# Longer activation and weight buffers, and one half of a layer in products of 256 columns

## The chip, the core and the metric

The kernel runs on one core of a Trainium2 chip. It is one program: a transformer block with adaptive normalization, then two layers of a second model, on 512 tokens of 1,024 features. The metric is the time of one execution on the device in microseconds (us). Three runs of the kernel before took 1934.53, 1937.00 and 1937.11 us; the median is 1937.0 us.

## The reference

Everything is float32. `x` is [512, 1024] after dropping the batch of one, and all weights come from memory.

```python
# block one: adaptive norm, two attentions, gates, an MLP
h      = modulate(rmsnorm(x, norm1_g), shift1, scale1)
proj   = h @ w_in                                  # 1024 -> 4352
merged = sigmoid(ga) * (swa(qa, ka, va) @ w_a) + sigmoid(gb) * (moba(qb, kb, vb) @ w_b)
x      = x + gate1 * (merged @ w_out)
h2     = modulate(rmsnorm(x, norm2_g), shift2, scale2)
x      = x + gate2 * (square(relu(h2 @ w_mlp_in)) @ w_mlp_out)   # 1024 -> 4096 -> 1024
x      = rmsnorm(x, final_g)
# block two: two layers
for layer in range(2):
    h = rmsnorm(x, mix_norm_g[layer])
    x = x + (even_mixer(h) if layer == 0 else odd_mixer(h))      # ends in a 1024 x 1024 product
    h = rmsnorm(x, mlp_norm_g[layer])
    x = x + square(relu(h @ mlp_w1[layer])) @ mlp_w2[layer]      # 1024 -> 4096 -> 1024
```

The three MLPs are most of the arithmetic: each has 64 tiles of 128 output features over 1,024 inputs.

## The kernel before

**Split products.** A float32 operand is written as a high part in the matmul's rounded format (`F32R`) and the rest as a low part: weights as `wH` and `wL`, activations as `aH` and `aL` (features on the partitions, 512 tokens along the row). `mm3` (line 198) issues three matmuls for each piece of 128 inputs: high weights by high activations, high weights by low activations, low weights by high activations. The weights are the stationary operand (128 columns, loaded before every matmul), the activations move through (512 columns).

**The loop of a product.** `gemm_t_steps` (line 212) goes over output tiles of 128 features. For each it loads a block of weights (`load_w`, line 178: a DMA into `wraw`, a copy on ScalarE into `wH`, a subtraction on VectorE into `wL`, three buffers of each), takes an accumulator `acc` in PSUM (three of them) and runs over eight pieces of inputs: 24 matmuls. Then the accumulator is evacuated. In two places the 512 tokens go by halves, in matmuls of 256 columns: in the first three tiles of the first MLP, and in the last tile of two products (`apart`). In the projections to keys and values (`gemm_n_steps`, line 246) the operands change places: the weights move and the activations stand still.

**The MLP** (`mlp`, line 828) has four chunks, `c` from 0 to 3. In each the first product makes eight hidden tiles from `H` (the tiles `aH0` to `aH7` and `aL0` to `aL7`); `ev` (line 834) applies relu and square and splits the result into two tiles of the pool `hd` (22 buffers). The second product takes these sixteen `hd` tiles and adds into the residual. So a chunk is 192 matmuls that read `aH` and `aL`, and then 192 that read `hd`. The MLP of block one is called at line 660, those of block two from `sq_mlp` (line 874, `layer` 0 and 1).

**What sets the order.** Within each engine the order is fixed when the program is built. TensorE takes its instructions in that order, and a load of weights goes ahead beside the matmul before it. In most of block one and in the mixers small attention matmuls are woven in among the long products by a planner with estimated times; in the MLPs there is nothing of that kind after the first 24 steps.

**Where the tiles lie.** Tiles lie at the same address in each of the 128 partitions. Counted modulo 256 bytes, the built program has them so (a tile of 512 float32 is 2,048 bytes long, a weight buffer 4,096, so all the buffers of a pool have one place):

| tiles | place before, modulo 256 |
|---|---|
| `aH0`-`aH7`, `aL0`-`aL7`, all `wH`, all `wL` | 128 |
| `hd` in the three MLPs | 64 |
| `s2` and `oh` in block one (inputs of the products `w_out`, `w_a`, `w_b`), and `S` and `PT`, which hold three blocks of weights in the first projections | 64 |
| `s2` in the last mixer: high part of the input of `od_out` | 224 |
| `v` in the last mixer: low part of that input; these buffers are 2,080 bytes apart | 224, 192, 160, 128, 96, 64, 32, 0 |

A slice of 128 weight columns or of 256 tokens begins at a multiple of 512 bytes, so it has the place of its tile.

Of the kernel before, what the change touches and what calls it, by code (L numbers as in the profile page):

```python
# [11 lines left out]
F32 = mybir.dt.float32  # L12
# [13 lines left out]
NEG = -1e30  # L26
LAT = 6.5
# [24 lines left out]
class Weave:  # L52
    """Places small dependent work on TensorE among the steps of long matrix products.

    A task is a generator: it emits one stage, then yields the TensorE time (us, estimated)
    before which its next stage should not stand in TensorE's queue, or a function that
    gives that time, or None while it isn't known."""
# [57 lines left out]
class Build:  # L115
# [62 lines left out]
    def load_w(self, src, n=1024, pools=None, pool_h=False, pool_l=False):  # L178
        nc = self.nc
        (hp, hn, hb), (lp, ln, lb) = pools or ((self.wp, "wH", 3), (self.wp, "wL", 3))  # L180
        r = self.wp.tile([P, 1024], F32, name="wraw", bufs=4)
        nc.sync.dma_start(r[:, :n], src)
        h = hp.tile([P, 1024], F32R, name=hn, bufs=hb)
        if pool_h:
            nc.gpsimd.tensor_scalar(h[:, :n], r[:, :n], 1.0, 0.0, op0=OP.mult, op1=OP.add)
        else:
            nc.scalar.activation(h[:, :n], r[:, :n], AF.Copy)  # L187
        l = lp.tile([P, 1024], F32R, name=ln, bufs=lb)
        (nc.gpsimd if pool_l else nc.vector).tensor_tensor(l[:, :n], r[:, :n], h[:, :n], op=OP.subtract)  # L189
        return h, l  # L190
# [21 lines left out]
    def gemm_t_steps(self, srcs, xs, evac, group=1, kt=KT, pool_l=(), ks=None, halves=False, last=None):  # L212
        """out^T tile m = W[:, 128 m:]^T x^T; srcs: one block [128, kt*128] per tile.

        halves: the first group goes over one half of the tokens first; last: evacuates the
        last tile instead of evac, half by half."""
        m = 0
        while m < len(srcs):
            g = group if m == 0 else 1
            ms = list(range(m, min(m + g, len(srcs))))  # L220
            ws = [self.load_w(srcs[i], kt * P, pool_l=i in pool_l or self.lean) for i in ms]
            accs = [self.acc() for _ in ms]
            lag = (0, 0, 3)
            ks = ks or range(kt)
            apart = last is not None and ms == [len(srcs) - 1]
            for c in HALVES if apart or (halves and m == 0) else (slice(0, NT),):
                if apart and c.start:
                    accs = [self.acc()]
                if c.start and not apart:
                    lag = (0, 3, 6)  # L230
                for _, b, i in sorted((i + lag[b], b, i) for i in range(kt) for b in range(len(ms))):
                    k = ks[i]
                    while xs[k] is None:
                        yield "wait"
                    s = slice(k * P, k * P + P)
                    h, l = ws[b]
                    self.mm3(accs[b][:, c], h[:, s], l[:, s], xs[k][0][:, c], xs[k][1][:, c], i == 0, i == kt - 1)
                    yield
                if apart:
                    last(c, accs[0])  # L240
            for i, acc in zip(ms, accs):
                if not apart:
                    evac(i, acc)
            m += len(ms)

    def gemm_n_steps(self, srcs, xs, evac):
        """out tile [128 tokens, 512] = x W; srcs: four blocks [128, 2 k tiles, 512]."""
        accs = [self.acc() for _ in range(3)] + [self.pg()]
        mm = self.mm
        for b in range(4):  # L250
            h, l = self.load_w(srcs[b], pool_l=self.lean)
            for i in range(4):
                t = slice(i * P, i * P + P)
                for kk in range(2):
                    k = 2 * b + kk
                    s = slice(kk * NT, kk * NT + NT)
                    xh, xl = xs[k]
                    mm(accs[i], xh[:, t], h[:, s], start=(k == 0), stop=False)
                    mm(accs[i], xl[:, t], h[:, s], start=False, stop=False)
                    mm(accs[i], xh[:, t], l[:, s], start=False, stop=(k == KT - 1))  # L260
                    yield
        for i in range(4):
            evac(i, accs[i])

    def act_hl(self, k):
        return (self.ap.tile([P, NT], F32R, name=f"aH{k}"), self.ap.tile([P, NT], F32R, name=f"aL{k}"))
# [6 lines left out]
    def rsqrt(self, out, a, eps):  # L273
        """out = (a + eps) ** -0.5 by Newton steps; small tiles, a may lie in PSUM."""
# [13 lines left out]
    def sumsq(self, src, k, tag="ssq", scale=1.0, apart=False):  # L288
        """adds the squares of tile k (features on partitions) to a running tile, or returns them."""
        nc = self.nc  # L290
        if k == 0:
            s = self.sm.tile([P, NT], F32, name=tag, bufs=1)
            nc.scalar.activation(s, src, AF.Square, scale=scale)
            self.cur[tag] = s
        else:
            q = self.sm.tile([P, NT], F32, name="sq", bufs=2)
            nc.scalar.activation(q, src, AF.Square, scale=scale)
            if apart:
                return q
            nc.vector.tensor_tensor(self.cur[tag], self.cur[tag], q, op=OP.add)  # L300

    def mean_rows(self, *parts, pool=None):
        """mean over features as PSUM [128, 512], the same in every partition."""
# [5 lines left out]
    def rstd_rows(self, ms, name="R"):  # L309
        """(ms + eps) ** -0.5 as SBUF [128, 512]."""  # L310
# [6 lines left out]
    def cols_of(self, R, pool=None):  # L317
        """[128 tokens, 4] columns of rows that are the same in every partition."""
# [8 lines left out]
    def modulate(self, x, k, R, A, shift, hl=None, c=slice(0, NT)):  # L327
        """x R A + shift of tile k, split."""
# [26 lines left out]
def block_one(B):  # L355
    nc, tc, a = B.nc, B.tc, B.a
    with ExitStack() as st:
# [25 lines left out]
        def ada_first(c):  # L383
            """128 columns of shift1 and of scale1, four row tiles at a time side by side on TensorE."""
# [16 lines left out]
        def ada_vec(c):  # L401
            """the same columns on VectorE."""
# [8 lines left out]
        def ada(part, cb):  # L411
            """512 columns of the modulation, on VectorE."""
# [41 lines left out]
        def ev_q(tiles, acc):  # L454
            """1/8 of two heads of 64 rows, each block of 128 queries back to front: for each head
            a tile with the high part in the head's own rows and the low part in the other ones."""
# [8 lines left out]
        def ev_k(tiles, acc):  # L465
            """for each of two heads a tile with the high part twice; the low parts of both in a third one."""
# [68 lines left out]
        def ev_g(m, acc):  # L535
            """sigmoid as exp(-ln(1 + exp(-x)))."""
# [43 lines left out]
        def ev_last(c, acc):  # L580
            """the last tile of the residual, by halves."""
# [60 lines left out]
    with ExitStack() as st:  # L642
        hp = st.enter_context(tc.tile_pool(name="hp", bufs=1))
        at = hp
        B.tmp = lambda: hp.tile([P, NT], F32, name="hd", bufs=22)
# [17 lines left out]
def flip_blocks(t):  # L663
    """columns of [128, 512] with each block of 128 back to front."""
# [3 lines left out]
def load_strips(B, at):  # L668
    """bucket of each distance as one-hot columns with the mask's rows, and the heads' biases."""
# [8 lines left out]
def bias_strips(B, at, oh):  # L678
    """masked bias by reversed distance, one row per head, in DRAM."""
# [10 lines left out]
def bias_tile(B, at, h, off, n):  # L690
    """[128 queries, n] additive bias of head h, already masked; the last query first."""
# [7 lines left out]
class Attention:  # L699
    """the two softmax attentions of block one, as tasks; heads share buffers, counted in free."""  # L700
# [18 lines left out]
    def head(self, key, h, b, q, k, strip, spans, qk_banks, pt_banks, times, sink=None):  # L719
        """P^T of one head; spans: first and last key of each query tile; banks: tiles that share a PSUM bank."""  # L720
# [107 lines left out]
def mlp(B, hp, w1, w2, H, upd, group=1, pool_l=(), during=None, mid=None, last=None):  # L828
    """during: called with each step's number in the first product, which goes over half of the tokens first; mid: called after it."""
    nc = B.nc  # L830
    for c in range(4):
        hs = []

        def ev(m, acc):
# [3 lines left out]
            hl = (hp.tile([P, NT], F32R, name="hd", bufs=22), hp.tile([P, NT], F32R, name="hd", bufs=22))  # L838
            B.split(hl, r)
            hs.append(hl)  # L840
        first = dict(group=group, pool_l=pool_l, halves=during is not None) if c == 0 else {}
        for i, _ in enumerate(B.gemm_t_steps([w1[c * 8 + m] for m in range(8)], H, ev, **first)):
# [3 lines left out]
        if mid is not None and c == 0:  # L846
            mid()
        B.gemm_t([w2[c * 8 + m] for m in range(8)], hs, lambda m, acc: upd(m, acc, c == 3),
                 last=last if c == 3 else None)
# [24 lines left out]
def sq_mlp(B, layer):  # L874
    nc, tc, a, X = B.nc, B.tc, B.a, B.X
    with ExitStack() as st:
# [24 lines left out]
        mlp(B, hp, a[f"mlp1_{layer}"], a[f"mlp2_{layer}"], H, upd, group=3, mid=norm, last=end if layer else None)  # L901


def even_mixer(B, ev, H):
# [11 lines left out]
    def stats():  # L916
        """rstd of both norms, and the end of the first one."""
# [56 lines left out]
    def gelu(t):  # L974
        """t <- gelu(t), tanh form: t * exp(-ln(1 + exp(-2 u)))."""
# [85 lines left out]
    def stick_head(j, b, As):  # L1061
        """A^T of one head, key tiles side by side, masked."""
# [27 lines left out]
    def split_y():  # L1090
        """parts of the result take the place of H once that is used up."""
# [37 lines left out]
def stick_scores(B, ev, q, k, z, h, l, tiles):  # L1129
    """masked scores of some key tiles, and log(1 + exp) of them in two parts."""  # L1130
# [22 lines left out]
def stick_weights(B, z, h, l, tiles):  # L1153
    """z <- exp(z - the sum over this key and the later ones), for some key tiles."""
# [285 lines left out]
```

## Time and profile before

| what | value |
|---|---|
| median of three runs | 1937.0 us |
| the same runs, lowest and highest | 1934.53 and 1937.11 us |
| span of the profiled execution, first to last instruction | 1936.0 us |
| instructions in it | 22136 |
| TensorE matmuls | busy 1898.4 us, 8570 matmuls |
| TensorE weight loads | busy 1501.6 us |
| VectorE, ScalarE, GpSimd | busy 1066.2, 767.3, 212.5 us |
| DMA | 197.43 MB, mean 102 GB/s |

No time of its own is listed for the profiled execution beside its span. The span of 1936.0 us lies 1.0 us under the median of the runs.

Two things have to be known to read the rows. Matmuls are pipelined, and the end of one is modelled: the duration of a matmul of 512 columns is shown as about 0.39 us, but the next one starts after some 0.23 us. What a matmul costs in a long product is therefore read from start to start, not from its duration. And a matmul in float32 that isn't of the rounded format is two matmuls in the trace.

### The profile page before, as it was taken

To read this page: it belongs to the slowest core of one execution; us is meant where nothing else is said; L and a number is where in the kernel's file an instruction comes from. 1 tells how busy PE (TensorE), PEld (TensorE's weight loads), DVE (VectorE), ACT (ScalarE), POOL (GpSimd) and SP (SyncE) were. 2 spreads that over 40 slices of the span, in tenths; PEclk is the share of its full clock that TensorE was granted. 3 is DMA by queue.
4 is the path that set the end of the run, shared out by engine and by line. 5 is a ranking of instruction groups with operands and counts; after the bars stand their busy time and mean duration, and the time that the engine had idled before them with its cause. 6 is when DMAs were issued, how large, how long until landed. Compare 5 with 4: busy or idle time off the path is not lost.

```text
span 1936.0 us, 22136 instructions
## 1 busy us (share of the span) xinstructions
PE 1898.4 (98%) x8570; PEld 1501.6 (78%) x8570; DVE 1066.2 (55%) x1571; ACT 767.3 (40%) x1246; POOL 212.5 (11%) x149
## 2 busy tenths in 40 slices
PE   6999999999999999999899999999999999999999
PEld 3777778888888887776688888888777888888887
DVE  4765668664434346667755445546745554454544
ACT  2455454342323244666634232233436343223231
POOL 1000010010000001325320201100201001210100
PEclk8999999999999999999999999999999999999999
DMA  6523258522223223211122322222231233223221
GB/s 233 165 55 104 89 170 261 188 88 89 97 98 98 89 96 115 66 55 55 44 88 98 98 92 96 96 98 90 89 108 44 77 101 106 97 89 98 98 98 66
DMA packets 61640, 197.43 MB, mean 102 GB/s; under 512 B 6904, under 2 KB 8490, under 8 KB 61536
## 3 DMA queue, kind: packets, MB, share of 16 engines
q1 hardware_dynamic: 57864, 190.34, 29.8%
q10 hardware_dynamic: 3672, 5.69, 1.1%
q8 instruction: 67, 1.10, 0.2%
q14 instruction: 37, 0.30, 0.1%
HBM read 193.86 MB, written 2.15 MB: 101 GB/s over the span
## 4 chain that ended last, share of the span: by engine, by line
PE 88%; DVE 7%; ACT 3%; issue 1%; DMA 1%; SPq 0%; DVEq 0%; ACTq 0%
PE acc L193 79%; PE pm L193 5%; PE pg L193 2%; PE po L193 1%; DVE s L1230 1%; DVE sl L1150 1%; PE pm L196 1%; DMA oh<-ada 1%; ACT wH L187 0%; DVE wL L189 0%; ACT sz L1168 0%; ACT se L1146 0%; ACT se L1147 0%; DVE ge L979 0%; DVE aL L335 0%
## 5 line engine op out<-in xcount | busy, mean ns | idle before, releaser
L187 ACT ACTIVATE wH<-wraw 128x1024 fp32r<-128x1024 f32 (+1 forms) x304 | 314.7, 1037 | 752.3 <-PE acc L193 683.0
L189 DVE TENSOR_TENSOR wL<-wraw,wH 128x1024 fp32r<-128x1024 f32 (+1 forms) x269 | 365.1, 1358 | 298.9 <-ACT wH L187 291.9
L193 PE MATMUL acc<-aH,wH 128*128 128x512 f32 (+1 forms) x1296 | 507.3, 392 | 5.5 <-ACT aH L334 5.0
L193 PE MATMUL acc<-aL,wH 128*128 128x512 f32 (+1 forms) x1296 | 502.2, 387 | 3.4 <-DVE aL L335 3.4
L193 PE MATMUL acc<-aH,wL 128*128 128x512 f32 (+1 forms) x1296 | 501.5, 387 | 0.0
L193 PE MATMUL acc<-hd,wH 128*128 128x512 f32 (+1 forms) x1552 | 483.2, 392 | 0.0
L193 PEld LDWEIGHTS acc<-hd,wH 128*128 128x128 f32 x1552 | 289.4, 187 | 70.8 <-issue 1.0
L193 PE MATMUL acc<-hd,wL 128*128 128x512 f32 (+1 forms) x776 | 304.0, 392 | 0.0
L193 PEld LDWEIGHTS acc<-aH,wH 128*128 128x128 f32 x1296 | 244.2, 189 | 62.7 <-issue 9.2
L193 PEld LDWEIGHTS acc<-aL,wH 128*128 128x128 f32 x1296 | 244.4, 189 | 53.8 <-DVE aL L335 4.3
L193 PEld LDWEIGHTS acc<-aH,wL 128*128 128x128 f32 x1296 | 244.4, 189 | 50.7 <-issue 1.2
L193 PEld LDWEIGHTS acc<-hd,wL 128*128 128x128 f32 x776 | 145.2, 187 | 35.2
L189 POOL TENSOR_TENSOR wL<-wraw,wH 128x1024 fp32r<-128x1024 f32 x38 | 96.2, 2536 | 675.7 <-ACT wH L187 654.7
L889 POOL TENSOR_TENSOR X<-X,up 128x512 f32<-128x512 f32 x48 | 69.9, 1456 | 573.2 <-DVE up L887 322.0
L887 DVE TENSOR_TENSOR up<-acc,R 128x512 f32<-128x512 f32 x63 | 43.6, 692 | 153.7 <-PE acc L193 153.7
L270 ACT ACTIVATE hd<-rl 128x512 fp32r<-128x512 f32 x96 | 60.6, 632 | 120.5 <-DVE rl L837 120.4
L271 DVE TENSOR_TENSOR hd<-rl,hd 128x512 fp32r<-128x512 f32 x96 | 66.3, 692 | 60.8 <-ACT hd L270 60.8
L655 DVE SCALAR_TENSOR_TENSOR X<-acc,mod,X 128x512 f32<-128x512 f32 x32 | 24.0, 751 | 88.9 <-PE acc L193 88.9
L193 PE MATMUL acc<-s,wH 128*128 128x512 f32 (+1 forms) x208 | 66.6, 379 | 0.0
L837 DVE TENSOR_TENSOR rl<-rl,acc 128x512 f32<-128x512 f32 x96 | 65.1, 681 | 0.0
L193 PE MATMUL pm<-s,s 64*128 64x384 f32 (+7 forms) x160 | 55.7, 436 | 0.0
L836 ACT ACTIVATE rl<-acc 128x512 f32<-128x512 f32 x96 | 55.4, 580 | 0.0
(312 smaller groups left out, 1917.6 us busy)
## 6 DMA issues: line engine op xcount, KB each, us to landing
wraw<-mlp SPq DMA_DIRECT2D x128, 512.0 KB, 3.2
wraw<-w SPq DMA_DIRECT2D x64, 512.0 KB, 3.2
wraw<-ada SPq DMA_DIRECT2D x32, 512.0 KB, 4.5
wraw<-w_in SPq DMA_DIRECT2D x30, 512.0 KB, 3.5
oh<-ada SPq DMA_DIRECT2D x32, 256.0 KB, 4.8
wraw<-od_in SPq DMA_DIRECT2D x16, 512.0 KB, 3.3
wraw<-ev_in SPq DMA_DIRECT2D x12, 512.0 KB, 3.3
X<-x SPq DMA_DIRECT2D x16, 256.0 KB, 4.6
```

Source lines behind the costliest of these rows:

```text
L187: nc.scalar.activation(h[:, :n], r[:, :n], AF.Copy)
L189: (nc.gpsimd if pool_l else nc.vector).tensor_tensor(l[:, :n], r[:, :n], h[:, :n], op=OP.subtract)
L193: self.weave.placed(self.nc.tensor.matmul(out, w, x, start=start, stop=stop), out, x)
L196: self.weave.placed(self.nc.tensor.transpose(out, x, self.ident[:x.shape[0], :x.shape[0]]), out, x)
L270: nc.scalar.activation(hl[0], src, AF.Copy)
L271: nc.vector.tensor_tensor(hl[1], src, hl[0], op=OP.subtract)
L655: nc.vector.scalar_tensor_tensor(X[m], acc, mod[:, 40 + m:41 + m], X[m], op0=OP.mult, op1=OP.add)
L836: nc.scalar.activation(r, acc, AF.Relu)
L837: nc.vector.tensor_tensor(r, r, acc, op=OP.mult)
L887: nc.vector.tensor_tensor(t, acc, R2, op=OP.mult)
L889: eng.tensor_tensor(X[m], X[m], t, op=OP.add)
L1150: nc.vector.tensor_tensor(l[:, c], e[:, :w], h[:, c], op=OP.subtract)
```

## The change

Two things are changed, and what is computed stays the same.

First, buffers become 32 bytes (`PAD` = 8 elements) longer: all `aH` and `aL`, the `wH` and `wL` of the pool `wp`, and the `hd` tiles. Only the added end is unused; every tile is read and written as before. Buffers that follow each other then begin 32 bytes further on modulo 256. In the built program:

| tiles | place after, modulo 256 |
|---|---|
| `aH0`-`aH7` | 128, 192, 0, 64, 128, 192, 0, 64 |
| `aL0`-`aL7` | 160, 224, 32, 96, 160, 224, 32, 96 |
| `wH`, three buffers | 128, 160, 192 |
| `wL`, three buffers | 224, 0, 32 |
| `hd` | all eight multiples of 32 |
| `s2` and `oh` of block one, `S` and `PT` | 0 |
| `s2` in the last mixer | 160 |
| `v` in the last mixer | all eight multiples of 32, as before |

Second, in the MLP of layer 0 of block two, the chunks `c` = 1 and 2 go by halves of the tokens: both products of these chunks run over eight pieces of inputs for tokens 0 to 255, and then again for tokens 256 to 511, in matmuls of 256 columns. Evacuation stays whole.

```diff
+PAD = 8
...
-        h = hp.tile([P, 1024], F32R, name=hn, bufs=hb)
+        w = 1024 + (PAD if hp is self.wp else 0)
+        h = hp.tile([P, w], F32R, name=hn, bufs=hb)
...
-        l = lp.tile([P, 1024], F32R, name=ln, bufs=lb)
+        l = lp.tile([P, w], F32R, name=ln, bufs=lb)
...
-            for c in HALVES if apart or (halves and m == 0) else (slice(0, NT),):
+            for c in HALVES if apart or halves == "all" or (halves and m == 0) else (slice(0, NT),):
...
     def act_hl(self, k):
-        return (self.ap.tile([P, NT], F32R, name=f"aH{k}"), self.ap.tile([P, NT], F32R, name=f"aL{k}"))
+        return tuple(self.ap.tile([P, NT + PAD], F32R, name=f"a{p}{k}")[:, :NT] for p in "HL")
...
-        B.tmp = lambda: hp.tile([P, NT], F32, name="hd", bufs=22)
+        B.tmp = lambda: hp.tile([P, NT + PAD], F32, name="hd", bufs=22)[:, :NT]
...
-def mlp(B, hp, w1, w2, H, upd, group=1, pool_l=(), during=None, mid=None, last=None):
+def mlp(B, hp, w1, w2, H, upd, group=1, pool_l=(), during=None, mid=None, last=None, apart=False):
...
-            hl = (hp.tile([P, NT], F32R, name="hd", bufs=22), hp.tile([P, NT], F32R, name="hd", bufs=22))
+            hl = tuple(hp.tile([P, NT + PAD], F32R, name="hd", bufs=22)[:, :NT] for _ in range(2))
...
+        if apart and c in (1, 2):
+            first = dict(halves="all")
...
-                 last=last if c == 3 else None)
+                 last=last if c == 3 else None, halves="all" if apart and c in (1, 2) else False)
...
-        mlp(B, hp, a[f"mlp1_{layer}"], a[f"mlp2_{layer}"], H, upd, group=3, mid=norm, last=end if layer else None)
+        mlp(B, hp, a[f"mlp1_{layer}"], a[f"mlp2_{layer}"], H, upd, group=3, mid=norm, last=end if layer else None, apart=layer == 0)
```

VectorE, ScalarE, GpSimd and the DMA queues have the same instructions in the same order before and after. On TensorE the order differs in the two chunks alone. The first place is TensorE in the first product of chunk 1: the end of the first output tile (`acc_8336`) and what follows. The numbers are those of the buffers.

```order
L193 MATMUL acc_8336<-aL6_7742,wH_8332 128x512
L193 MATMUL acc_8336<-aH6_7741,wL_8334 128x512
L193 MATMUL acc_8336<-aH7_7745,wH_8332 128x512
L193 MATMUL acc_8336<-aL7_7746,wH_8332 128x512
L193 MATMUL acc_8336<-aH7_7745,wL_8334 128x512
L193 MATMUL acc_8374<-aH0_7717,wH_8370 128x512
L193 MATMUL acc_8374<-aL0_7718,wH_8370 128x512
```

The same place after the change:

```order
L195 MATMUL acc_8336<-aL6_7742,wH_8332 128x256
L195 MATMUL acc_8336<-aH6_7741,wL_8334 128x256
L195 MATMUL acc_8336<-aH7_7745,wH_8332 128x256
L195 MATMUL acc_8336<-aL7_7746,wH_8332 128x256
L195 MATMUL acc_8336<-aH7_7745,wL_8334 128x256
L195 MATMUL acc_8336<-aH0_7717,wH_8332 128x256
L195 MATMUL acc_8336<-aL0_7718,wH_8332 128x256
```

After the eighth piece the same tile begins again at the first piece, for the other 256 tokens; the matmuls are half as wide, and there are twice as many.

The second place is TensorE in the second product of chunk 1, whose inputs are the hidden tiles. The last hidden tile is `hd_8630` (high) and `hd_8631` (low) before; its matmuls are the 22nd to 24th of the first output tile (`acc_8640`).

```order
L193 MATMUL acc_8640<-hd_8630,wH_8636 128x512
L193 MATMUL acc_8640<-hd_8631,wH_8636 128x512
L193 MATMUL acc_8640<-hd_8630,wL_8638 128x512
L193 MATMUL acc_8674<-hd_8364,wH_8670 128x512
L193 MATMUL acc_8674<-hd_8365,wH_8670 128x512
L193 MATMUL acc_8674<-hd_8364,wL_8672 128x512
```

After the change the last hidden tile is `hd_8822` and `hd_8823`, the first output tile `acc_8832` and the second `acc_8890`:

```order
L195 MATMUL acc_8890<-hd_8512,wL_8888 128x256
L195 MATMUL acc_8832<-hd_8822,wH_8828 128x256
L195 MATMUL acc_8890<-hd_8574,wH_8886 128x256
L195 MATMUL acc_8890<-hd_8575,wH_8886 128x256
L195 MATMUL acc_8890<-hd_8574,wL_8888 128x256
L195 MATMUL acc_8890<-hd_8636,wH_8886 128x256
L195 MATMUL acc_8890<-hd_8637,wH_8886 128x256
L195 MATMUL acc_8832<-hd_8823,wH_8828 128x256
L195 MATMUL acc_8832<-hd_8822,wL_8830 128x256
```

There, 21 matmuls of the first tile's first half come first, then 9 of the second tile, then the first that reads the last hidden tile's high part, 5 more of the second tile, and then the one that reads its low part.

## Rows read from the trace of the kernel before

**Rows 1.** The page: busy time, granted clock in 40 slices, shares of the chain.

```profile
PE 1898.4 (98%) x8570; PEld 1501.6 (78%) x8570; DVE 1066.2 (55%) x1571; ACT 767.3 (40%) x1246; POOL 212.5 (11%) x149
...
PEclk8999999999999999999999999999999999999999
...
PE acc L193 79%; PE pm L193 5%; PE pg L193 2%; PE po L193 1%; DVE s L1230 1%; DVE sl L1150 1%; PE pm L196 1%; DMA oh<-ada 1%; ACT wH L187 0%; DVE wL L189 0%; ACT sz L1168 0%; ACT se L1146 0%; ACT se L1147 0%; DVE ge L979 0%; DVE aL L335 0%
```

**Rows 2.** Stretches: length, busy PE, PEld, DVE, ACT, POOL (count), clock, DMA, GB/s.

```profile
410.00:762.00 352.00, 352.00 (x1590) 289.20 (x1589) 162.85 (x196) 120.19 (x160) 4.79 (x2) 1.00 0.29 95
762.00:968.00 206.00, 195.36 (x883) 139.16 (x881) 139.66 (x208) 128.91 (x241) 71.62 (x34) 0.97 0.19 62
...
1366.00:1497.00 131.00, 127.64 (x569) 98.16 (x568) 77.43 (x166) 66.94 (x136) 17.08 (x25) 1.00 0.22 74
```

**Rows 3.** Groups of matmuls by shape: out<-operands, shapes, count | busy us, mean ns.

```profile
L193 PE MATMUL acc<-aH,wH 128*128 128x512 f32 x1248 | 493.3, 396 | 5.1 <-ACT aH L334 4.7 <-DVE X L461 0.4
L193 PE MATMUL acc<-aL,wH 128*128 128x512 f32 x1248 | 488.4, 391 | 0.9 <-DVE aL L335 0.9
L193 PE MATMUL acc<-aH,wL 128*128 128x512 f32 x1248 | 487.9, 391 | 0.0
L193 PE MATMUL acc<-hd,wH 128*128 128x512 f32 x1520 | 477.7, 395 | 0.0
L193 PE MATMUL acc<-hd,wL 128*128 128x512 f32 x760 | 299.6, 394 | 0.0
L193 PE MATMUL acc<-s,wH 128*128 128x512 f32 x176 | 60.6, 396 | 0.0
L193 PE MATMUL acc<-wH,aH 128*128 128x512 f32 x120 | 50.2, 419 | 1.8 <-DVE cp L1226 1.8
L193 PE MATMUL acc<-s,wL 128*128 128x512 f32 x120 | 47.5, 396 | 0.0
...
L193 PE MATMUL acc<-oh,wH 128*128 128x512 f32 x128 | 40.9, 401 | 0.0
L193 PE MATMUL acc<-oh,wL 128*128 128x512 f32 x64 | 25.3, 395 | 0.0
L193 PE MATMUL acc<-v,wH 128*128 128x512 f32 x64 | 25.2, 394 | 0.0
...
L193 PE MATMUL pg<-wH,aH 128*128 128x512 f32 x40 | 16.5, 412 | 0.0
```

**Rows 4.** Stretches, TensorE: chunk 1 of layer 0, both products (192 matmuls each).

```profile
1096.08:1139.62 43.54, 43.54 (x193) 1.00 0.31 102
1139.62:1184.42 44.80, 44.80 (x193) 1.00 0.27 89
```

**Rows 5.** TensorE in order of time, `od_out`: start, duration; 24 matmuls lie between.

```profile
1553.09 0.39 PE L193 MATMUL acc<-s,wH 128*128 128x512 f32 x1
...
1558.69 0.39 PE L193 MATMUL acc<-s,wH 128*128 128x512 f32 x1
```

**Rows 6.** The same view, first projections with weights in `S`, `PT`: 9 matmuls lie between.

```profile
64.39 0.39 PE L193 MATMUL pg<-aH,S 128*128 128x512 f32 x1
...
66.45 0.40 PE L193 MATMUL acc<-aH,wH 128*128 128x512 f32 x1
```

**Rows 7.** The same view, halves over `aH`, `aL` in block one's MLP: 9 matmuls.

```profile
405.61 0.28 PE L193 MATMUL acc<-aH,wL 128*128 128x256 f32 x1
...
406.69 0.28 PE L193 MATMUL acc<-aH,wL 128*128 128x256 f32 x1
```

**Rows 8.** The same view, halves over `hd`, the kernel's last tile: 42 matmuls.

```profile
1927.47 0.28 PE L193 MATMUL acc<-hd,wL 128*128 128x256 f32 x1
...
1932.23 0.28 PE L193 MATMUL acc<-hd,wL 128*128 128x256 f32 x1
```

**Rows 9.** ScalarE, then VectorE in order of time: chunk 1's last hidden tile.

```profile
1142.59 0.63 ACT L270 ACTIVATE hd<-rl 128x512 fp32r<-128x512 f32 x1 [1.40 <-DVE rl L837]
...
1143.26 0.69 DVE L271 TENSOR_TENSOR hd<-rl,hd 128x512 fp32r<-128x512 f32 x1 [0.70 <-ACT hd L270]
```

## Prediction

> **What bounds the kernel now.** I read the page first: TensorE is busy for 1898.4 of 1936.0 us, and matmuls into `acc` alone are 79% of the chain that ended last [rows 1]. The clock row shows full speed in every slice but the first. By stretches, TensorE is busy without a gap from 410 to 762 us, at clock 1.00; it idles for 10.6 us in the even mixer (762 to 968) and for 3.4 us in the first part of the odd one (1366 to 1497) [rows 2]. So nearly everywhere the time is the number of matmuls times the interval from the start of one to the start of the next, and transfers, VectorE and ScalarE follow TensorE.
>
> That interval isn't the same everywhere. Both products of chunk 1 in layer 0 are 192 matmuls of 512 columns: the first, over `aH` and `aL`, takes 43.54 us, or 226.8 ns each, the second, over `hd`, 44.80 us, or 233.3 ns each [rows 4]. Clock, engine, form and count are the same. At the granted clock of 1.00, the 2.4 GHz level, 512 columns are 213.3 ns, so 13 ns and 20 ns are lost per matmul. By the table of places, moving and stationary operand lie at 128 and 128 modulo 256 in the first product, at 64 and 128 in the second.
>
> Two other pairings are in the trace. With the moving operand at 128 and the weights at 64, 9 matmuls take 2.06 us: 228.9 ns [rows 6]. In `od_out` the high part lies at 224, the low part at all eight places in turn, the weights at 128: 24 matmuls take 5.60 us, 233.3 ns [rows 5]. At 256 columns the order turns round: 9 matmuls over `aH`/`aL` take 1.08 us, 120.0 ns, and 42 over `hd` take 4.76 us, 113.3 ns [rows 7, 8]. Two halves over `hd` thus cost 226.7 ns, less than one whole matmul; two over `aH` cost 240.0, more.
>
> **The change part by part.** *Longer buffers.* They add no instruction; they change pairings. The pairing 128/128, which has the shortest interval of 512 columns in these rows, becomes a mix: `aH` at four places, `aL` at four others, the weights at three and three. The products over `hd` become a mix of all eight. No row shows both operands mixed. From below, the nearest rows give 226.7 ns, from above I allow 235, a little over the highest row, since two mixed sides may cost more than one. `od_out`, with one side mixed, gives 233.3 and the pairing 128/64 gives 228.9. I take 232, nearer to `od_out`, because its low parts pass through all eight differences to the weights, the equal place and a distance of 64 among them, and the sum comes out no better than the fixed pairing of `hd`. I can't tell what in the pairing costs the time, only that the one that is left behind has the lowest interval.
>
> The Trainium skill ("SBUF — State Buffer", section "Who interferes with whom") says that TensorE has two independent read ports, for the moving operand and for weights, and that it never waits on anyone. By that, places would be worth nothing. The trace disagrees as far as it goes: 226.8 and 233.3 ns for the same form at the same clock. What the time would be if places didn't matter is the third case below.
>
> The sum, at 232 ns:
> - over `aH`/`aL`: 3 x 1248 matmuls [rows 3], less 384 that go by halves: 3360 x (232 - 226.7) = +17.8 us;
> - with the weights moving: 3 x 120 and 3 x 40 matmuls [rows 3], 480 x 5.3 = +2.5;
> - over `hd`: 1520 + 760 [rows 3] less 384: 1896 x (232 - 233.3) = -2.5;
> - over `s`, `oh` and `v`: 176 + 120 + 128 + 64 + 64 = 552 [rows 3], taken at 233.3 as in rows 5: 552 x -1.3 = -0.7.
>
> Some of this is covered. In the mixers' two stretches with idle time, 20 tiles of 24 matmuls and four products of 96 with the weights moving read `aH`/`aL`, 864 x 5.3 = 4.6 us; where TensorE waits for ScalarE or VectorE there, a longer matmul only shortens the wait. I take 1.8 us off (bounds 0 and 4.6).
>
> *Halves.* In two chunks, 2 x 192 matmuls over `aH`/`aL` and 2 x 192 over `hd` become twice as many of 256 columns. Known intervals are 113.3 and 120.0 [rows 7, 8]; for a mix I take the middle, 116.7, two being 233.4. Against 226.8 that is 384 x 6.6 = +2.5; against 233.3 it is 0. Bounds: -2.6 us for both at 113.3, +7.7 at 120.0. Each weight load is now used for half as many columns, but at 113.3 ns the loads keep up already.
>
> At the hand-over to the second product the last hidden tile is wanted earlier. Its high part was done at 1143.22 us and its low part at 1143.95 [rows 9], 3.60 and 4.33 us after TensorE began the second product at 1139.62 [rows 4]. Before, 21 matmuls of 233.3 ns stand ahead of it, 4.90 us. After, 30 of 116.7 ns (3.50 us) stand ahead of the high part and 36 (4.20 us) ahead of the low one, since the order puts 14 matmuls of the second tile in between. Everything on TensorE queues behind a wait there. I take 0.3 us per chunk, +0.6 in all; bounds 0 and 1.5.
>
> VectorE and ScalarE have the same work in the same order and wait for TensorE in these stretches; longer rows cost them nothing as far as the rows can show. Transfers are the same bytes.
>
> Together: 17.8 + 2.5 - 2.5 - 0.7 - 1.8 + 2.5 + 0.6 = +18.4 us on the span of 1936.0, so 1954.4, and with the 1.0 us by which the median lies above the span, **1955 us**. With the mixed interval at 229.5 ns the same sum gives about 1941, at 234.5 about 1971: the own range of this case.
>
> **The rivals.** *The mix is better than either fixed pairing.* If the 233.3 ns of `hd` comes from a fixed pairing that meets itself in every matmul, spreading the places breaks it: `hd`, `s`, `oh` and `v` fall to 226.7 (2448 x -6.6 = -16.2 us), `aH` stays, the halves run at 113.3 (-2.6): -18.8, 1918 us. For it: 128/64 with its 228.9 ns shows that being unequal needn't cost 6.6 ns [rows 6]. Against: `od_out` is spread on one side and stands at 233.3 [rows 5]. It decides below a common interval of 228.9 ns: there 3840 matmuls lose as much as 2448 and the halves gain.
>
> *The whole loss goes.* If unequal places keep the two reads apart altogether, intervals approach the 213.3 ns of the clock: 3840 x 13.4 + 2448 x 20 + 384 x 13.4 + 384 x 20 = -113 us at the limit; half of it gives 1880. For it: something costs 13 to 20 ns per matmul, and it differs by place. Against: no stretch in rows 4 to 6 is under 226 ns, and three of their four pairings are unequal. The Trainium skill ("TensorE: Matmul & The Clock Gate", section "Wait — 56ns, not 53.3ns?") gives N ÷ 2.4 GHz plus about 2.5 ns between back-to-back matmuls, 215.7 ns at 512 columns; an estimate from that page, with every matmul at it, is 94 us less, about 1843 us. No long product of this trace runs at that interval.
>
> *Places are not the cause.* The difference in rows 4 may belong to something else that goes with the tiles, and the buffers' length does nothing. Then only the halves count: 384 x (240.0 - 226.8) = +5.1, 384 x (226.7 - 233.3) = -2.5, +0.6 for the hand-over: 1940 us. For it: I know places from the program, not from the trace. Against: the input of `od_out` comes from another pool and other engines than `hd` and has the same 233.3 ns.
>
> **How the numbers follow.** A measurement of this kernel can tell about 0.2% from no change, 1933 to 1941 us. Forecast (a mix near 232 ns, slower): 0.67. Mix better than either: 0.17. The whole loss goes: 0.07. Places not the cause: 0.09, within the bound. So faster 0.24, same 0.09, slower 0.67. The range of 8 in 10 reaches from 1918, the first rival, to 1972, a mix of 234.5 ns, and leaves out the second rival and a mix worse than any row. The likeliest case alone spans 1941 to 1971.
>
> **What would show it.** In the profile after: the first products of chunks 0 and 3 of layer 0 should take 44.5 us per 192 matmuls where 43.54 stood; their second products 44.5 where 44.80 stood; chunks 1 and 2, both products, 44.8 each, at intervals of some 117 ns. The MLP of layer 1, which has no halves, should show the buffers' effect alone, 192 x (5.3 - 1.3) = 0.8 us more per chunk. `od_out` should stay at 233. At the hand-over a wait of TensorE for `hd` of some tenths should appear. I am wrong if the products over `aH` stay at 226.7 or fall below, if those over `hd` fall to 227, or if an interval near 215 ns shows up anywhere; and if ScalarE or VectorE instructions on longer rows change their durations, which I take as unchanged.

## The result and the profile after

The changed kernel takes 1954.2 us (median of four runs, 1953.57 to 1956.37), the kernel before in the same runs 1937.05. The ratio is 1.0083, with a 95% interval of 1.0065 to 1.0101: slower, near the predicted 1955.

The page after, span and engines (busy us, share of the span, count):

```profile
span 1951.7 us, 23684 instructions
...
PE 1917.5 (98%) x9338; PEld 1543.3 (79%) x9338; DVE 1064.1 (55%) x1571; ACT 767.6 (39%) x1246; POOL 213.4 (11%) x149
```

Against [rows 1], TensorE is busy for 19.1 us more in 15.7 us more of span; the granted clock is full from the second slice on, as before. The 768 added matmuls are the halves of 768 long ones. VectorE, ScalarE and GpSimd have their old counts and within 2.1 us their old busy times, so the longer rows did not change their instructions.

Where the span grew is read from stretches with the same work on both sides. Columns: start and end, length, busy TensorE (count, with the one to three matmuls that reach over an edge), clock, DMA share, GB/s. Cuts lie where a long product begins. The kernel before, nine stretches in a row:

```profile
0.00:452.28 452.28, 432.14 (x2130) 0.99 0.46 148
452.28:762.10 309.82, 309.82 (x1345) 1.00 0.29 94
762.10:1050.89 288.79, 278.15 (x1247) 0.98 0.22 72
1050.89:1096.08 45.19, 45.19 (x194) 1.00 0.28 88
1096.08:1272.76 176.68, 176.68 (x769) 1.00 0.29 96
1272.76:1361.10 88.34, 88.34 (x385) 1.00 0.28 93
1361.10:1533.50 172.40, 169.04 (x753) 1.00 0.25 83
1533.50:1578.29 44.79, 44.79 (x193) 1.00 0.28 94
1578.29:1926.89 348.60, 348.60 (x1515) 1.00 0.28 92
```

The changed kernel, the same nine, and then chunks 1 to 3 of layer 0 product by product:

```profile
0.00:455.43 455.43, 436.30 (x2130) 0.99 0.45 147
455.43:767.05 311.62, 311.62 (x1346) 1.00 0.28 94
767.05:1056.55 289.50, 280.39 (x1248) 0.98 0.22 72
1056.55:1101.47 44.92, 44.92 (x194) 1.00 0.27 89
1101.47:1283.27 181.80, 181.66 (x1537) 1.00 0.28 94
1283.27:1372.26 88.99, 88.99 (x386) 1.00 0.28 92
1372.26:1546.48 174.22, 171.86 (x753) 1.00 0.25 82
1546.48:1590.98 44.50, 44.50 (x194) 1.00 0.29 95
1590.98:1942.42 351.44, 351.44 (x1515) 1.00 0.27 92
...
1101.47:1146.70 45.23, 45.23 (x385) 1.00 0.31 99
1146.70:1192.26 45.56, 45.49 (x387) 1.00 0.27 89
1192.26:1237.47 45.21, 45.21 (x386) 1.00 0.29 98
1237.47:1283.27 45.80, 45.73 (x386) 1.00 0.26 89
1283.27:1327.78 44.51, 44.51 (x194) 1.00 0.30 99
1327.78:1372.26 44.48, 44.48 (x193) 1.00 0.27 86
```

In order, the stretches grow by 3.15, 1.80, 0.71, -0.27, 5.12, 0.65, 1.82, -0.29 and 2.84 us, and the end by 0.17: 15.7 us in all. A third lies in the fifth, the two chunks that go by halves. The last two lines against [rows 4] (chunk 3 has the same products as chunk 1) show the longer buffers alone: the product over `aH` and `aL` goes from 43.54 to 44.51 us per 192 matmuls (226.8 to 231.8 ns), that over `hd` from 44.80 to 44.48 (233.3 to 231.7). Both meet near 232 ns, and the first kind is the one that loses. `od_out` too comes to 44.50, that is 231.8 ns. The four products by halves take 45.2 to 45.8 us, more than either whole form.

At the hand-over in chunk 1, ScalarE on the high part of the last hidden tile (start, duration, in brackets the idle time before and what ended it), to be set beside [rows 9], and TensorE at that time:

```profile
1149.79 0.63 ACT L272 ACTIVATE hd<-rl 128x512 fp32r<-128x512 f32 x1 [1.40 <-DVE rl L841]
...
1150.12 0.28 PE L195 MATMUL acc<-hd,wL 128*128 128x256 f32 x1
1150.47 0.62 PE L195 MATMUL acc<-hd,wH 128*128 128x256 f32 x3
```

The high part is done at 1150.42 us, 3.72 us after the second product began. TensorE starts its next matmul 0.05 us later, 0.35 us after the one before where 0.12 is usual: it waited for that tile, and lost 0.23 us. The stretch view shows only 0.07 us of this as idle (45.56 - 45.49), since the modelled end of the matmul before covers the rest. In chunk 2 it is 0.07 again.

### The profile page after: what moved, and what is told of

Its sections match the earlier page's. It is cut to its first block, busy times and chain, and to the rows that moved or that the text cites. A ratio compares the mean times of both kernels' runs of the same rounds, so it can differ in the third digit from the quotient of the medians.

```text
span 1951.7 us, 23684 instructions
## 1 busy us (share of the span) xinstructions
PE 1917.5 (98%) x9338; PEld 1543.3 (79%) x9338; DVE 1064.1 (55%) x1571; ACT 767.6 (39%) x1246; POOL 213.4 (11%) x149
## 4 chain that ended last, share of the span: by engine, by line
PE 89%; DVE 6%; ACT 3%; issue 1%; DMA 0%; SPq 0%; DVEq 0%; ACTq 0%
PE acc L195 79%; PE pm L195 6%; PE pg L195 2%; PE po L195 1%; DVE s L1236 1%; PE pm L198 1%; DVE sl L1156 1%; DVE wL L191 1%; ACT wH L189 0%; DMA X<-x 0%; DVE aL L337 0%; DVE ssq L302 0%; DVE ge L985 0%; ACT ge L988 0%; DVE s L991 0%
## 5 line engine op out<-in xcount | busy, mean ns | idle before, releaser
L195 PE MATMUL acc<-aH,wH 128*128 128x512 f32 (+1 forms) x1424 | 535.4, 377 | 5.3 <-ACT aH L336 5.0
L195 PE MATMUL acc<-aL,wH 128*128 128x512 f32 (+1 forms) x1424 | 529.5, 372 | 3.7 <-DVE aL L337 3.7
L195 PE MATMUL acc<-aH,wL 128*128 128x512 f32 (+1 forms) x1424 | 527.6, 371 | 0.0
L195 PE MATMUL acc<-hd,wH 128*128 128x512 f32 (+1 forms) x1808 | 493.0, 361 | 0.1
L195 PEld LDWEIGHTS acc<-hd,wH 128*128 128x128 f32 x1808 | 320.8, 188 | 56.8 <-issue 1.0
L195 PE MATMUL acc<-hd,wL 128*128 128x512 f32 (+1 forms) x904 | 325.1, 360 | 0.0
L195 PEld LDWEIGHTS acc<-aH,wH 128*128 128x128 f32 x1424 | 269.2, 189 | 62.2 <-issue 9.2
L195 PEld LDWEIGHTS acc<-aL,wH 128*128 128x128 f32 x1424 | 269.6, 189 | 52.6 <-DVE aL L337 4.4
L195 PEld LDWEIGHTS acc<-aH,wL 128*128 128x128 f32 x1424 | 269.1, 189 | 51.0 <-issue 1.2
L195 PEld LDWEIGHTS acc<-hd,wL 128*128 128x128 f32 x904 | 169.9, 188 | 27.8
```

What stands on the lines that cost most here:

```text
L195: self.weave.placed(self.nc.tensor.matmul(out, w, x, start=start, stop=stop), out, x)
```

## The experiments

The leading theory: the interval of a matmul is set by how far its weights lie from its moving operand, modulo 256 bytes. I call that the difference, weights minus moving. In the kernel before it is 0 over `aH` and `aL`, 64 over `hd`; in the changed kernel it takes all eight multiples of 32. Rivals: the moving operand's place alone, the length of the buffers, or the halves.

**Each part alone.** The changed kernel without the halves (`...` stands for what is left out):

```diff
-mlp(B, hp, ..., last=end if layer else None, apart=layer == 0)
+mlp(B, hp, ..., last=end if layer else None)
```

> The longer buffers without the halves. Theory of places (the interval of a 512-column product is set by where its moving and its weight operand lie to each other modulo 256 bytes): all MLP chunks of layer 0 take 44.5 us per 192 products as those of layer 1 do in the changed kernel, so the four products that went by halves (45.2 to 45.8 us) win back 0.7 to 1.3 us each, together about 3.7 us: about 1950.5 us. Rival, that the order by halves makes the loss: at or below 1937 us.

And the kernel before with the halves in chunks 1 and 2 of layer 0, no buffer longer:

```diff
+            for c in HALVES if apart or halves == "all" or (halves and m == 0) else (slice(0, NT),):
...
+        if apart and c in (1, 2):
+            first = dict(halves="all")
...
+                 last=last if c == 3 else None, halves="all" if apart and c in (1, 2) else False)
...
```

> The halves without the longer buffers. Theory of places: a pair of 256-column products on part H/L tiles of the activation costs 2 x 120.0 = 240.0 ns against 226.7 ns for one of 512 columns, on hidden tiles 2 x 113.3 = 226.7 ns against 233.3 ns; 2 x 192 x 13.3 ns = +5.1 us and 2 x 192 x -6.7 ns = -2.6 us, with 0.6 us at the two hand-overs +3.1 us: about 1940 us, first product of chunk 1 about 46.1 us and second about 43.5 us. Rival, that the halves make the loss: about 1954 us. Rival, that the halves are worth their cost only with the longer buffers: the same 1954 us.

The longer buffers alone: 1952.1 us, ratio 1.0064 (1.0049 to 1.0080), where about 1950.5 was expected. The halves alone: 1944.4 us, ratio 1.0033 (1.0019 to 1.0046), where about 1940 was. Both parts lose, the buffers most of it. Chunks 1 and 2, each with both products, with the longer buffers alone (44.5 us per product, as expected):

```profile
1102.17:1191.23 89.06, 89.06 (x386) 1.00 0.29 95
1191.23:1280.31 89.08, 89.08 (x385) 1.00 0.29 95
```

The same chunks with the halves alone, by product:

```profile
1093.94:1140.01 46.07, 46.07 (x385) 1.00 0.29 97
1140.01:1185.60 45.59, 45.41 (x387) 1.00 0.27 89
1185.60:1231.67 46.07, 46.07 (x387) 1.00 0.29 96
1231.67:1277.25 45.58, 45.40 (x387) 1.00 0.27 89
```

On mixed places the halves cost 181.80 - 178.14 = 3.7 us (the fifth stretch after, less these two), on the places before 183.31 - 176.68 = 6.6 us. The first products came as expected (46.1: two matmuls of 120.0 ns). The second did not: 45.6 where 43.5 was expected. TensorE in order of time in the second product of chunk 1, halves alone, shows where (start, duration; x3 is three matmuls):

```profile
1140.26 0.28 PE L193 MATMUL acc<-hd,wL 128*128 128x256 f32 x1
...
1143.32 0.28 PE L193 MATMUL acc<-hd,wL 128*128 128x256 f32 x1
1143.78 0.62 PE L193 MATMUL acc<-hd,wH 128*128 128x256 f32 x3 [0.18 <-ACT hd L270]
...
1184.07 0.28 PE L193 MATMUL acc<-hd,wL 128*128 128x256 f32 x1
...
1185.48 0.28 PE L193 MATMUL acc<-hd,wL 128*128 128x256 f32 x1
```

From 1140.26 to 1143.32 us lie 27 matmuls, 113.3 ns each, as in [rows 8]. Then TensorE waits for the last hidden tile (0.46 us from start to start where 0.11 is usual), and at the product's end 12 matmuls take 1.41 us: 117.5 ns each. The pools of the operands, their places and the clock are the same. So the 113.3 ns that I took from 42 matmuls at the kernel's end isn't what a whole product takes; after that wait the stream ran at the other interval. That the wait is what changed it is only argued.

**Difference or place.** The kernel before with gaps of 64 bytes, first ahead of the hidden tiles (the difference over `hd` becomes 0), then, with the halves in it, ahead of the activation parts (every tile moves, the differences stay):

```diff
+        nc.vector.memset(self.sm.tile([P, 16], F32, name="gap_sm"), 0.0)
...
+        nc.vector.memset(self.cn.tile([P, 16], F32, name="gap_cn"), 0.0)
```

The first line is the first kernel's, the second the second kernel's; the lines of the halves are left out.

> The kernel before with a gap of 64 bytes ahead of the buffers of hidden tiles, so that hidden tiles stand at 128 modulo 256 like the weights; lengths and order as before. Theory of places: hidden-tile products of 512 columns go from 233.3 to 226.7 ns, 2280 x 6.67 ns = -15.2 us, the 192 on oh -1.3 us, about half of 192 on s -0.6 us: about 1920 us, each second product 43.5 us per 192. Rival, that the length of the buffers sets it, not the place: 1937 us, 44.8 us. Rival, that mixing places is what is slow or fast and no fixed place differs: 1937 us.

> The halves alone, with a gap of 64 bytes ahead of the activation parts, so that activation parts, weights and hidden tiles all stand 64 higher modulo 256 and their differences stay as in the kernel before. Theory of the difference of the two places: as the kernel with the halves alone, 43.5 us per 192 products on activation parts and 44.8 us on hidden tiles, chunk 1 46.1 and 43.5 us. Rival, that the place of the moving operand alone decides (best at 128, as the activation parts in the kernel before): hidden tiles, now at 128, take 43.5 us per 192, and activation parts, now at 192, more than 43.5 us.

The first takes 1920.6 us, ratio 0.9905 (0.9892 to 0.9918): 1.0% faster than the kernel before. About 1920 was expected; that it came out so close is partly luck, since the median of the kernel before was 1940.25 us beside this run and 1937 in the expectation. The spans of the two profiled executions, both at a mean clock of 0.994, are 1936.0 and 1918.1 us: 17.9 us apart, where 17.1 were reckoned. Its chunk 1, both products, then `od_out`, whose operands this gap doesn't bring together:

```profile
1085.22:1128.74 43.52, 43.52 (x194) 1.00 0.31 103
1128.74:1172.26 43.52, 43.52 (x194) 1.00 0.28 91
1520.32:1565.04 44.72, 44.72 (x193) 1.00 0.28 95
```

The second, with activation parts now at 192 and hidden tiles at 128: a product over `aH` and `aL`, then one over `hd`.

```profile
585.64:629.18 43.54, 43.54 (x193) 1.00 0.29 97
629.18:673.98 44.80, 44.80 (x193) 1.00 0.29 94
```

Hidden tiles at 128 with the weights at 192 keep their 44.80 us; activation parts at 192 keep 43.54. The place of the moving operand alone is out; its difference to the weights decides. In one run it took 1942.1 us, beside 1944.4 for the halves alone. Its chunk 1 by halves took 46.07 and 45.58 us; the 43.5 that I expected of the second product failed here as with the halves alone.

**Length.** The `hd` buffers 256 bytes longer, so that every tile keeps its place modulo 256:

```diff
-        B.tmp = lambda: hp.tile([P, NT], F32, name="hd", bufs=22)
+        B.tmp = lambda: hp.tile([P, NT + 64], F32, name="hd", bufs=22)[:, :NT]
...
+            hl = tuple(hp.tile([P, NT + 64], F32R, name="hd", bufs=22)[:, :NT] for _ in range(2))
```

> The kernel before with the buffers of hidden tiles 256 bytes longer, so that each is longer but stands where it did modulo 256. Theory of places: 233.3 ns and 44.8 us per second product as before, the time of the kernel before within 0.2%. Rival, that the greater length itself changes the interval (as in the changed kernel, 231.6 to 232.0 ns on hidden tiles): 44.5 us per second product, 6 x 0.3 us less.

Chunk 1, both products, unchanged (1936.2 us in one run, beside 1941.5 for the kernel before, whose own runs spread as far):

```profile
1094.46:1138.00 43.54, 43.54 (x194) 1.00 0.30 102
1138.00:1182.80 44.80, 44.80 (x194) 1.00 0.27 90
```

Buffers that follow each other now lie 2,304 bytes apart, so a step of a whole 256 bytes changes nothing either: counting modulo 256 is enough for these tiles. Steps of less than 32 bytes were not tried.

**All eight differences.** Three kernels with the halves, and gaps of 32, 128 or 224 bytes ahead of the weights and of 224, 160 or 128 ahead of the hidden tiles:

```diff
+        nc.vector.memset(self.wp.tile([P, 8], F32, name="gap_wp"), 0.0)
...
+        nc.vector.memset(self.sm.tile([P, 56], F32, name="gap_sm"), 0.0)
...
```

These are the first kernel's lines; the other two have 32 and 56 for the 8, and 40 and 32 for the 56.

> The halves alone, with gaps of 32 bytes ahead of the weights and 224 ahead of the hidden tiles: the weights stand 32 bytes after the activation parts modulo 256 and 96 after the hidden tiles, in every product. Two theories of why mixed differences take 232 ns. That each difference has its own interval and a mix takes the mean of them: differences 0, 64 and 192 take 226.7, 233.3 and 228.9 ns, so the five others must take 233.4 ns on the average, and 192 products 44.8 us. Rival, that a constant difference settles on a short interval and it is the change from one to the next that costs: 227 to 231 ns, 43.6 to 44.4 us per 192.

> As the run at differences 32 and 96, with the weights 128 bytes after the activation parts and 160 after the hidden tiles. Theory of a mean of fixed intervals: about 233.4 ns (44.8 us per 192 products) for both. Rival, that only changes of the difference cost: 227 to 231 ns (43.6 to 44.4 us). A third, that places count modulo 128 alone: 128 as 0, 226.7 ns and 43.5 us.

> As the run at differences 32 and 96, with the weights 224 bytes after the activation parts and 192 after the hidden tiles. Theory of a mean of fixed intervals: 224 about 233.4 ns (44.8 us per 192 products), 192 the 228.9 ns of the 9 products of S and PT before (43.9 us). Rival, that only changes of the difference cost: 227 to 231 ns for both. That places count modulo 128 alone: 192 as 64, 233.3 ns.

In one run each they took 1964.1, 1960.6 and 1949.6 us. In block one's MLP a product over `aH` and `aL` and then the next over `hd`: at differences 32 and 96,

```profile
501.94:546.74 44.80, 44.80 (x194) 1.00 0.29 94
546.74:591.71 44.97, 44.97 (x193) 1.00 0.29 94
```

at 128 and 160,

```profile
498.29:543.09 44.80, 44.80 (x194) 1.00 0.29 94
543.09:587.90 44.81, 44.81 (x194) 1.00 0.28 94
```

at 224 and 192:

```profile
500.56:545.36 44.80, 44.80 (x194) 1.00 0.28 94
545.36:589.30 43.94, 43.94 (x193) 1.00 0.29 96
```

| difference | 0 | 32 | 64 | 96 | 128 | 160 | 192 | 224 |
|---|---|---|---|---|---|---|---|---|
| ns for 512 columns (stretch / 192) | 226.7 | 233.3 | 233.3 | 234.2 | 233.3 | 233.4 | 228.9 | 233.3 |

Only 0 and, less, 192 are better than the rest. The 228.9 ns at 192 agree with the 9 matmuls of [rows 6]. The five that were not known average 233.5, against the 233.4 that a mean of fixed intervals asked for; the rival's 227 to 231 and the halving of the period to 128 bytes both fall. All eight average 232.05 ns, and the changed kernel, which goes through all eight, shows 231.7 to 231.8.

The agreement is in the total alone. Set beside the addresses of the built program matmul by matmul, the trace of the changed kernel shows that its matmuls at difference 0 don't take 226.7 ns: in unbroken runs of 512-column matmuls into `acc`, the 666 at difference 0 took 232.1 ns from start to start on the average, and the averages at all eight differences lie between 230.6 and 232.8. Counted by the weights of the matmul that follows, they lie between 230.6 and 234.0. So the good difference isn't good any more within a mix.

In chunk 1's first product, by halves, the three kernels show that another difference is the better one at 256 columns: 45.44 us at 32, 46.08 at 128, and at 224

```profile
1099.49:1144.29 44.80, 44.80 (x385) 1.00 0.30 102
```

against the 46.07 at 0 above.

**Is a mix a mean?** The kernel before with a gap between high and low weight parts, so that two matmuls of three stand at 0 and one at 64, over `aH` and over `hd` alike:

```diff
+        if lp is self.wp and not hasattr(self, "gap"):
+            self.gap = self.wp.tile([P, 16], F32, name="gap_wl")
+            nc.vector.memset(self.gap, 0.0)
```

> The kernel before with a gap of 64 bytes between the buffers of the high and of the low weight parts: high parts stand at difference 0 to activation parts and hidden tiles, low parts at 64, so that two products of three are at 0 and one at 64. Theory that a mix takes the mean of the fixed intervals: (2 x 226.7 + 233.3) / 3 = 228.9 ns, 43.95 us per 192 products, first and second products alike, about 1925 us. Rival, that each change of the difference costs by itself: over 233 ns, 44.8 us or more, about 1942 us or more.

```profile
498.54:542.91 44.37, 44.37 (x193) 1.00 0.29 95
542.91:587.28 44.37, 44.37 (x193) 1.00 0.29 95
```

44.37 us is 231.1 ns, between the two expectations, and neither held: a mix of two intervals costs 2.2 ns per matmul more than their mean of 228.9. One run took 1945.7 us, slower than the kernel before. By the starts in that trace, the matmuls of the low weight parts (difference 64) take 235.5 to 235.8 ns, where a constant 64 gives 233.3, and those of the high parts (0) take 228.4 to 229.3, where a constant 0 gives 226.7: all three pay some 2 ns, those that keep the difference of the matmul before them too. So the mean came out right for the changed kernel, but it isn't the rule; why a mix costs what it does is open.

**Everything together.** The gap of 64 bytes, and in the last mixer a gap of 96 bytes and `v` buffers of 2,304 bytes:

```diff
+        nc.vector.memset(self.sm.tile([P, 16], F32, name="gap_sm"), 0.0)
...
+    nc.vector.memset(od.tile([P, 24], F32, name="gap_od"), 0.0)
...
-        t = od.tile([P, 2, 257], F32, name="v", bufs=8)
+        t = od.tile([P, 576], F32, name="v", bufs=8)[:, :514].rearrange("p (a b) -> p a b", a=2)
...
```

> The kernel with the gap of 64 bytes ahead of the hidden tiles, and in the layer of od_out also a gap of 96 bytes and v buffers of 2304 bytes, so that every product of 512 columns on f32r parts (but 16 with the triangle of ones) has its weights and its moving operand at one place modulo 256. Theory of places: od_out goes from 44.72 to 43.52 us per 192, the rest stays: 1.2 us less than with the gap alone, about 1919.4 us. Rival, that od_out waits for something else: 1920.6 us and 44.7 us.

1920.7 us, ratio 0.9904 (0.9887 to 0.9920): no different from the gap alone. `od_out` did fall to the expected length; first the stretch that ends where the second product of layer 0's chunk 0 begins, then `od_out`:

```profile
947.96:1045.30 97.34, 93.89 (x419) 0.96 0.26 87
...
1524.40:1567.92 43.52, 43.52 (x193) 1.00 0.29 97
```

The same first stretch, from the same matmul on, in the kernel with the gap alone:

```profile
946.58:1041.25 94.67, 91.23 (x418) 1.00 0.27 89
```

In this execution the granted clock was 0.96 in a stretch where it was 1.00 there, and the stretch took 2.7 us more, which is more than the 1.2. The other three runs, 1919.15 to 1920.93 us, don't stand clear of the 1920.09 to 1921.02 with the gap alone either, so whether the whole kernel gains stays open.

## Why the prediction was right

The time was right, and so was the size of the main step. That 1955 and 1954.2 us lie so close is partly luck. By parts, the working's +18.4 us and the measured +15.7 of span:

| part | predicted | measured |
|---|---|---|
| MLP products of 512 columns outside the mixers' stretches | +5.7 | +5.2 |
| chunks 1 and 2 of layer 0 by halves, hand-over included | +3.1 | +5.1 |
| first projections, mixers, `od_out`, two first products in them, cover taken off | +9.6 | +5.4 |

Two terms missed in opposite directions, and the median lies 2.5 us above the profiled span (1954.2 against 1951.7) where I took 1.0; in the sum these nearly cancel.

- *The mixed interval of 232 ns* held: 231.7 and 231.8 in chunk 3, and 178.14 us for the 768 matmuls of chunks 1 and 2 with the longer buffers alone, 232.0. Layer 1's MLP grew by 2.84 us, 0.7 per chunk where 0.8 was forecast. Its reason was only that `od_out` also passes through all eight differences. The table bears out that few differences are good ones, but not that a mix averages them: a mix of 0 and 64 costs more than their mean, and the matmuls at difference 0 in the changed kernel took 232.1. So the size was right, and why it is 232 stays open. That `od_out` was the nearest row was luck in part: it fell to 231.8 itself, where the text let it stay at 233.
- *The halves* were mis-sized, by 2.0 us. I put a pair at 233.4 ns (2 x 116.7) and it took 235.6 in the first product (45.23 / 192) and 236.1 in the second (45.56 less the 0.23 of the wait, / 192). With the halves alone the second product ran at 118 ns from its 31st matmul on (1143.78 to 1185.60 us, 354 matmuls). So the fault lies with the 113.3 ns end of the middle: a figure from 42 matmuls at the kernel's end, taken for a steady one.
- *The hand-over* held: 0.23 us in chunk 1 where I took 0.3, and the high part done 3.72 us after the second product began, with 3.50 us of matmuls reckoned ahead of it.
- *The cover* was under-sized. In the three stretches with idle time TensorE's idle fell from 20.14, 10.64 and 3.36 us to 19.13, 9.11 and 2.36, by 3.5 us, where I took 1.8 (bound 4.6). Before cover 11.4 us were reckoned for that part and 5.4 came, so 6.0 were missing, more than the bound. The products with the weights moving show it: in their unbroken runs the median interval went from 227 to 232 ns, as forecast, but from start to start, waits included, their 480 matmuls took 117.4 us after 117.1, where 2.5 us more were reckoned. The rest isn't traced further.
- *Mix better than either*: fell. The common interval of 231.7 to 232.0 ns is above the 228.9 that was to decide. Its premise was that 64 is a bad pairing which spreading avoids; six of the eight differences take 233 to 234 ns, and `hd` gained 1.6 ns from the mix, not 6.6.
- *The whole loss goes*: fell. No stretch read here is under 226.7 ns. The Trainium skill ("TensorE: Matmul & The Clock Gate", section "Wait — 56ns, not 53.3ns?") gives 215.7 ns from start to start at 512 columns; against that, 11 ns per matmul are unexplained here even at difference 0.
- *Places are not the cause*: fell, by the two gaps and the longer `hd` buffers. The argument that I had against it was weaker than it reads: the input of `od_out` is split by the same engines as `hd`, ScalarE and VectorE, and lies only in other pools.

## What to carry over

Where a long product streams at a full clock and TensorE never idles, read its start-to-start interval per stretch; two products of one form with different intervals are worth asking about. Here the address of the tiles modulo 256 bytes decided, and one gap of 64 bytes that put the hidden tiles level with the weights gave 1.0%, where spreading the addresses alone cost 0.6%. Take an interval from a whole product, not from a few dozen matmuls, before multiplying it by hundreds.

## What the runs showed of the hardware

- For matmuls of 512 columns on operands in the rounded format, each with its own weight load, at a granted clock of 1.00, the interval depends on the two addresses together. Where weights minus moving operand, modulo 256 bytes, is the same in every matmul, it was 226.7 ns at 0, 228.9 at 192, and 233.3 to 234.2 at the other six multiples of 32. With both 64 bytes further on it stayed (43.54 and 44.80 us per 192).
- The Trainium skill ("SBUF — State Buffer", section "Who interferes with whom") has TensorE wait on nobody; these runs disagree for a pair of reads of TensorE's own, if that is what collides. Which step loses the time isn't shown.
- Two differences in turn cost more than their mean: 231.1 ns with two matmuls of three at 0 and one at 64, against 228.9.
- Matmuls of 256 columns on operands of the same pools and places ran at 113.3 ns and, later in the same product, at 117.5. Why isn't shown.
- At 256 columns difference 0 isn't the best: two halves at it took 240 ns (46.07 us per 192 pairs), against 226.7 for the whole; at 224 they took 233.3 (44.80 us).
